# A decoder trunk on one core: attention scores of two units issued by turns into two banks

## The chip, the cores and the metric

The kernel runs on one core of one Trainium2 chip. The metric is the device time of the whole program in microseconds (us). Three runs of the kernel before took 1552.73, 1553.09 and 1553.78 us; their median is 1553.09.

The core has engines that work side by side, each through its own list of instructions in a fixed order: PE (matrix products and transposes, with PEld for its weight loads), DVE (vectors), ACT (functions of one operand, copies), POOL, and SP, which here only issues DMA transfers. A result of PE lies in one of eight banks of PSUM, each 128 rows of 512 fp32 numbers, and has to be read from there by DVE or ACT. An engine that meets an instruction whose operand or whose bank is not ready waits, and all that is behind it in its list waits too.

## The reference

The program computes a trunk of two decoder layers for 256 tokens of 1024 numbers in fp32. Each layer has attention with two groups of eight heads, an output projection, and a feed-forward part: dense in layer 0, eight experts with the best two for each token in layer 1.

```python
for layer in range(DEPTH):
    u = rmsnorm(h, attn_norm[layer])
    proj = u @ w_in[layer]
    ...
    o_a = nsa_mixer(...)        # group A: compressed + selected + window branch, gated
    o_b = dilated_mixer(...)    # group B
    o = jnp.concatenate([rmsnorm(o_a, ...), rmsnorm(o_b, ...)], axis=-1)
    h = h + o @ w_out[layer]
    v = rmsnorm(h, ffn_norm[layer])
    h = h + (swiglu(...) if layer % 2 == 0 else moe_swiglu(...))
```

The scores of one head are the products of its 256 queries with its keys, 64 numbers each, plus a bias that depends on the distance; then comes exp, and the product with the values. In group A a head has two such branches with the same queries (selected and window), and a third one on 15 keys that come from a small network over windows of 32 tokens (the compression).

## The kernel before

The 256 tokens are two tiles t = 0, 1 of 128 rows. Weights come in pieces of 1 MB through four raw slots (`N_RAW`), in the order of one list (`Weights`, L94 and L95 split each half-piece into a high part `whi`, by ACT, and a low part `wlo`, by DVE). A slot is loaded again when its last reader has run. Products with weights are made of three fp32r products each (`product3`, L366 to L368): `pj` for the input projection, `y` for the output projection, `eg`, `eu`, `ey` for the experts.

`attention` makes the projections in chunks: three for group A, then three for group B (`B_CHUNKS`: keys, queries, values). Right behind the first chunk of group B the list of weights has the four pieces of `cmp_w1` (1 MB each), which the compression reads whole, unsplit.

A group is worked off in units (`branch`). A unit fills one bank with scores (`sc`): at t=0 four heads or branches of 128 keys, at t=1 two of 256 keys. Its front is, for each of the two or four, a sum with the bias and the row minimum on DVE (L481, into `ns`, with `mn`) and exp on ACT (L483). Its back is four transposes on PE (`pT`, L490) into a bank, and a copy to `pt`, by ACT and DVE in turn (L493, L495). Its last step is eight products with the values (`o`, L502). In group A two heads that share a unit's place differ in g, and head g reads the rows g*64 to g*64+63 of queries and keys; so units alternate between the halves of the rows. In group B it is r that alternates.

The banks of PSUM: three under the tag "mm" (projections), two under "tr" (all transposes, and the scores), two under "acc" (`o`), one under "cmp". The compression (`compress`, from L537) has its steps in "cmp": `xt` (transposes of keys and values, L541), eight additions `xp` on DVE (L549), `hid` (128 products into strips of 32 columns, L559), then `hidT`, `kvc`, `kcT`. `combine` (L510 to L527) scales a branch's output and adds it up in `oa`.

The program text is not the order of the engines. A scheduler walks through the steps by its own estimate of when each is ready and when a bank or a slot comes free, and writes each engine's list; where a tag has fewer banks than steps that want one, the step that comes first in the text gets it.

Of the kernel before, what the change touches and what calls it, by code (L numbers as in the profile page):

```python
# [2 lines left out]

# [7 lines left out]
F32 = mybir.dt.float32  # L11
# [10 lines left out]
S = 256  # L22
# [15 lines left out]
# columns of the packed constant array  # L38
C_ID, C_TRI, C_IOTA, C_BDM, C_VALID, C_END = 0, 128, 256, 386, 394, 396
# rows of the packed vectors  # L40
# [12 lines left out]
class Weights:  # L53
    """Weight tiles: loaded in the order of the list, fp32 in, an exact sum of two fp32r parts out."""
# [25 lines left out]
    def take(self):  # L80
        """The two parts of the next piece, for each of its blocks of 128 rows."""
# [5 lines left out]
        out = []  # L87
# [13 lines left out]
def trunk_kernel(ctx: ExitStack, tc: tile.TileContext, T: dict, out: bass.AP):  # L101
# [23 lines left out]
    BANKS_A = (tr_bank,)  # L125
    BANKS_B = (tr_bank, cmp_bank)

    # ---------------------------------------------------------------- weights
# [52 lines left out]
    # the experts' pieces also go where attention has finished  # L181
# [3 lines left out]
    # -------------------------------------------------------------- constants  # L185
# [64 lines left out]
    # ones, and ones where the row is before the column: exact in bf16  # L250
# [5 lines left out]
    # distance bias, negated, and the mask, as rows over distance + 255  # L256
    scr = dram.tile([16, 512], F32, name="scr")

    def bias_rows(apool):
        oh = apool.tile([32, 512], F32, name="oh", tag="ns", bufs=2)  # L260
        pool.dma_start(out=oh, in_=T["c_onehot"])
        cn = apool.tile([16, 512], F32, name="cn", tag="ns", bufs=2)
# [7 lines left out]
    # ---------------------------------------------------------------- helpers  # L270
    def rsqrt(ms, shape, name):
        """1/sqrt(ms), by Newton's steps from an integer guess."""
# [17 lines left out]
    def row_rstd(src, n, name):  # L290
        """rstd of each token over the n columns of src[t]."""
# [6 lines left out]
    def split_psum(hi, lo, src, scale=None):  # L298
        """src * scale = hi + lo, both fp32r."""
# [8 lines left out]
    def transpose_split(src, row, l, hi, lo, ks):  # L308
        """hi + lo [128, k, S] = gain * transpose of the column blocks of src[t], blocks ks of the gain."""
# [9 lines left out]
    def lift(row, l, c0, cw, hi, lo):  # L319
        """Columns c0 ... of h, transposed, for the product that follows the norm of this row."""  # L320
        ks = range(c0 // 128, (c0 + cw) // 128)
        k = slice(ks[0], ks[-1] + 1)
        transpose_split([h[t][:, c0:c0 + cw] for t in range(NT)], row, l, hi[:, k, :], lo[:, k, :], ks)

    def turn_h(c0, cw, ht):
        """Columns c0 ... of h, transposed."""
# [12 lines left out]
    def residual(c0, cw, y, scale=None):  # L339
        """Columns c0 ... of h += scale * y[t]."""  # L340
# [12 lines left out]
    def column_groups(c, fine):  # L353
        """The groups of columns in which half c of h is computed: smaller ones where the next phase waits for them."""
        return [(0, 256), (256, 256)] if fine and c == 1 else [(0, 512)]

    def out_banks(bank, cw):
        """One output of cw columns for each token tile."""
# [5 lines left out]
    def product3(dst, xh, xl, wh, wl, first, last):  # L364
        """dst += (xh + xl) (wh + wl) to fp32's accuracy."""
# [3 lines left out]

    def dense(dst, hi, lo, cw):  # L370
        """dst[t][:, :cw] = (hi + lo)^T @ the next two weight tiles."""
# [6 lines left out]
    # -------------------------------------------------------------- attention  # L378
    def attention(l, apool, hi, lo, following):
# [7 lines left out]
        # row p begins one column further on: the columns run from the last key to the first  # L387
# [10 lines left out]
        # the projections: of group A the queries, the rest; of group B the queries and keys, the values  # L398
# [14 lines left out]
        def head_rstd(src, n, name, scale=None):  # L413
            """rstd of each of the n heads of src[t], times scale."""
# [14 lines left out]
        def norm_heads(dst, pj, c0, name, paired=False):  # L429
            """The eight heads of dst[t], each scaled by its rstd; paired: heads i and 4 + i side by side."""  # L430
# [13 lines left out]
        def norm_keys():  # L444
            """The selected and the window keys of group A, scaled by their rstd, in place."""
# [8 lines left out]
        def heads_t(dst, pj, c0, n, scale):  # L454
            """dst [128, n, S], or its two parts: n pairs of heads of pj, transposed and scaled."""
# [13 lines left out]
        def branch(units, t, scores, vpj, tbl, banks):  # L469
            """Causal attention of the units: lists of (head, column of v, output, denominators)."""  # L470
# [3 lines left out]
            def front(u, k):  # L474
                b = banks[k % len(banks)]("sc")
# [657 lines left out]
```

## Time and profile before

| | |
|---|---|
| median of three runs | 1553.09 us |
| profiled execution, first to last instruction | 1555.6 us |
| PE busy | 1527.9 us (98%) |
| DVE, ACT busy | 1235.4 us (79%), 1026.8 us (66%) |
| mean granted clock of PE | 0.993 |
| read from memory | 433.92 MB |

The attention of layer 0 lies between about 20 and 165 us, that of layer 1 between about 390 and 525 us; from about 535 us on it is the experts. The granted clock is a share of full speed: 1.00 is 2.4 GHz, 0.50 is 1.2 GHz. The rows of the section below have the start and the length of a group of instructions in us; a product's shown length includes what the next one overlaps, so the time that it takes is read from its start to the start of the next. In square brackets stands how long the engine had been idle, and for what.

### The profile page before, as it was taken

The page shows a single profiled execution, that of the slowest core. Times are in us where ns is not written, and L with a number is a line of the kernel's source. Part 1 is how long each engine was busy: PE and PEld are TensorE (multiplying, and loading weights), DVE is VectorE, ACT ScalarE, POOL GpSimd, SP SyncE. Part 2 cuts the span into 40 slices and gives each one's busy share as a digit, 9 for nine tenths or more (in the row PEclk, how much of TensorE's full clock was granted, in tenths as well). Part 3 has the DMA queues.
Part 4 walks back from the last instruction along what each step waited for, and adds up shares of the span by engine and source line. Part 5 has one row for each costly group of instructions (what it writes and reads, how often), then busy time and mean ns, then how long its engine had stood idle before and what let it go on. Part 6 is the DMA issues. An engine that isn't in the chain of part 4 may idle for free.

```text
span 1555.6 us, 20636 instructions
## 1 busy us (share of the span) xinstructions
PE 1527.9 (98%) x7502; PEld 1234.2 (79%) x7502; DVE 1235.4 (79%) x1771; ACT 1026.8 (66%) x1389; POOL 7.8 (1%) x17
## 2 busy tenths in 40 slices
PE   7999999999999999999999999999999999999997
PEld 6767888888777888888888878887887887887885
DVE  5567755555766798998998888988888889888886
ACT  5445644445545587887787777767777776767774
POOL 2000000000000000000000000000000000000000
PEclk9999999999999999999999999999999999999999
DMA  8812455557626499999999989999999999999980
GB/s 263 292 55 82 157 178 177 200 189 234 229 96 217 167 357 331 379 357 329 361 363 333 363 320 336 344 356 342 326 370 352 327 358 346 329 352 365 353 323 29
DMA packets 200907, 436.94 MB, mean 281 GB/s; under 512 B 9448, under 2 KB 26080, under 8 KB 200800
## 3 DMA queue, kind: packets, MB, share of 16 engines
q1 hardware_dynamic: 198160, 434.63, 79.2%
q8 instruction: 61, 1.00, 0.3%
q10 hardware_dynamic: 2176, 0.52, 0.2%
q0 software_dynamic: 464, 0.40, 0.1%
q14 instruction: 46, 0.38, 0.1%
HBM read 433.92 MB, written 1.08 MB: 280 GB/s over the span
## 4 chain that ended last, share of the span: by engine, by line
PE 95%; DMA 2%; DVE 2%; ACT 1%; issue 1%; SPq 0%; ACTq 0%; DVEq 0%
PE eu L368 7%; PE eg L368 7%; PE eu L367 6%; PE eu L366 6%; PE eg L367 6%; PE eg L366 6%; PE ey L366 6%; PE ey L367 6%; PE ey L368 6%; PE pj L368 3%; PE pj L366 3%; PE pj L367 3%; PE y L368 2%; PE y L367 2%; PE y L366 2%; PE o L502 2%
## 5 line engine op out<-in xcount | busy, mean ns | idle before, releaser
L95 DVE TENSOR_TENSOR wlo<-raw,whi 128x1024 fp32r<-128x1024 f32 (+1 forms) x802 | 946.1, 1215 | 158.9 <-ACT whi L94 147.9
L94 ACT ACTIVATE whi<-raw 128x1024 fp32r<-128x1024 f32 (+1 forms) x802 | 807.0, 1051 | 188.7 <-PE y L367 45.2
L368 PE MATMUL eg<-wlo,xe 128*128 128x512 f32 x448 | 177.4, 396 | 1.5 <-DVE wlo L95 1.5
L368 PE MATMUL eu<-wlo,xe 128*128 128x512 f32 x448 | 178.6, 399 | 0.0
L366 PE MATMUL ey<-whi,eth 128*128 128x512 f32 x448 | 177.5, 397 | 0.7 <-ACT eth L301 0.7
L366 PE MATMUL eg<-whi,xe 128*128 128x512 f32 x448 | 176.8, 395 | 0.7 <-ACT xe L304 0.3
L366 PE MATMUL eu<-whi,xe 128*128 128x512 f32 x448 | 177.4, 396 | 0.0
L367 PE MATMUL ey<-whi,etl 128*128 128x512 f32 x448 | 176.8, 395 | 0.0
L367 PE MATMUL eg<-whi,xe 128*128 128x512 f32 x448 | 175.9, 393 | 0.0
L367 PE MATMUL eu<-whi,xe 128*128 128x512 f32 x448 | 175.2, 391 | 0.0
L368 PE MATMUL ey<-wlo,eth 128*128 128x512 f32 x448 | 165.7, 399 | 0.0
L368 PEld LDWEIGHTS eu<-wlo,xe 128*128 128x128 f32 x448 | 84.1, 188 | 23.9 <-DVE wlo L95 6.9
L368 PEld LDWEIGHTS eg<-wlo,xe 128*128 128x128 f32 x448 | 84.2, 188 | 22.4 <-DVE wlo L95 4.6
L366 PEld LDWEIGHTS ey<-whi,eth 128*128 128x128 f32 x448 | 84.3, 188 | 20.7 <-ACT eth L301 1.1
L367 PEld LDWEIGHTS ey<-whi,etl 128*128 128x128 f32 x448 | 84.5, 189 | 20.2 <-DVE etl L302 0.4
L366 PEld LDWEIGHTS eg<-whi,xe 128*128 128x128 f32 x448 | 84.2, 188 | 20.3 <-ACT whi L94 2.6
L367 PEld LDWEIGHTS eg<-whi,xe 128*128 128x128 f32 x448 | 84.1, 188 | 17.8
L367 PEld LDWEIGHTS eu<-whi,xe 128*128 128x128 f32 x448 | 84.2, 188 | 17.1
L366 PEld LDWEIGHTS eu<-whi,xe 128*128 128x128 f32 x448 | 84.2, 188 | 15.8
L368 PEld LDWEIGHTS ey<-wlo,eth 128*128 128x128 f32 x448 | 82.5, 188 | 17.4
L301 ACT ACTIVATE eth<-eT 128x512 fp32r<-128x512 f32 x56 | 33.1, 592 | 88.7 <-PE ey L368 75.0
L366 PE MATMUL pj<-whi,uhi 128*128 128x512 f32 (+1 forms) x192 | 76.3, 399 | 0.8 <-ACT qv L411 0.8
(299 smaller groups left out, 1970.5 us busy)
## 6 DMA issues: line engine op xcount, KB each, us to landing
raw<-in_exp_w_gate_dram SPq DMA_DIRECT2D x112, 1024.0 KB, 7.0
raw<-in_exp_w_up_dram SPq DMA_DIRECT2D x112, 1024.0 KB, 7.0
raw<-in_exp_w_down_dram SPq DMA_DIRECT2D x112, 1024.0 KB, 6.8
raw<-in_w_in_dram SPq DMA_DIRECT2D x20, 1024.0 KB, 6.0
raw<-in_ffn_w_gate_dram SPq DMA_DIRECT2D x10, 1024.0 KB, 5.1
raw<-in_ffn_w_up_dram SPq DMA_DIRECT2D x10, 1024.0 KB, 5.2
raw<-in_ffn_w_down_dram SPq DMA_DIRECT2D x10, 1024.0 KB, 5.1
raw<-in_cmp_w_dram SPq DMA_DIRECT2D x8, 1024.0 KB, 6.2
```

The lines of the kernel that those rows point to most:

```text
L94: self.nc.scalar.activation(hi[:, :m * w], src, AF.Copy)
L95: self.nc.vector.tensor_tensor(out=lo[:, :m * w], in0=src, in1=hi[:, :m * w].bitcast(F32), op=ALU.subtract)
L301: act.activation(hi, src, AF.Copy)
L366: pe.matmul(dst, xh, wh, start=first, stop=False)
L367: pe.matmul(dst, xl, wh, start=False, stop=False)
L368: pe.matmul(dst, xh, wl, start=False, stop=last)
L502: pe.matmul(o[:, hd * HD:(hd + 1) * HD], pt[:, c:c + 128], vpj[:, j, vc:vc + HD], start=(j == 0), stop=(j == nj - 1))
```

## The change

Units are taken in pairs. The scores of both are issued first, step by step by turns, one unit into a bank of "tr" and the other into "cmp", for group A as for group B; then come both fronts, then for each unit its back and its last step. Group A's scores had "tr" alone before. The two units of a pair lie in different halves of the rows. `ns` has four buffers instead of two. The count of instructions of each kind stays the same, and so do their sizes.

```diff
-    BANKS_A = (tr_bank,)
+    BANKS_A = (tr_bank, cmp_bank)
...
+    def product3_by_steps(dst, xh, xl, wh, wl):
+        yield partial(pe.matmul, dst, xh, wh, start=True, stop=False)
+        yield partial(pe.matmul, dst, xl, wh, start=False, stop=False)
+        yield partial(pe.matmul, dst, xh, wl, start=False, stop=True)
...
-            def front(u, k):
-                b = banks[k % len(banks)]("sc")
-                ns = apool.tile([128, 512], F32, name="ns", tag="ns", bufs=2)
+            def products(us, k):
+                bs = [banks[(k + i) % len(banks)]("sc") for i in range(len(us))]
+                for step in zip(*[scores(b, u) for b, u in zip(bs, us)]):
+                    for mm in step:
+                        mm()
+                return bs
+
+            def front(u, b):
+                ns = apool.tile([128, 512], F32, name="ns", tag="ns", bufs=4)
                 mn = apool.tile([128, 4], F32, name="mn", tag="mn", bufs=3)
-                scores(b, u)
...
-            for k, u in enumerate(units):
-                _, ns = front(u, k)
-                last(u, back(ns, k))
+            for k in range(0, len(units), 2):
+                us = units[k:k + 2]
+                fronts = [front(u, b) for u, b in zip(us, products(us, k))]
+                for i, u in enumerate(us):
+                    last(u, back(fronts[i], k + i))
```

`scores` yields its products now instead of issuing them, in group A by `product3_by_steps`. The new lines move all line numbers behind them; L485 of the new kernel is the line that issues the scores.

What the scheduler makes of it is shown at three places of PE's list in layer 0. The first is the first scores of group A, before (`sc_513` is the bank of the first unit, `pj_1024` a bank of the first projection of group B):

```order
L366 MATMUL pj_1024<-whi_1029,uhi_93 128x512
L367 MATMUL pj_1024<-whi_1029,ulo_94 128x512
L368 MATMUL pj_1024<-wlo_1030,uhi_93 128x512
L366 MATMUL sc_513<-kta_425,qta_424 128x256
L367 MATMUL sc_513<-kta_425,qta_424 128x256
L366 MATMUL pj_1024<-whi_1029,uhi_93 128x512
L368 MATMUL sc_513<-kta_425,qta_424 128x256
```

and after (`sc_513` is the unit in "tr", `sc_514` its partner):

```order
L368 MATMUL pj_1024<-whi_1057,ulo_94 128x512
L485 MATMUL sc_513<-kta_425,qta_424 128x256
L485 MATMUL sc_514<-kta_425,qta_424 128x256
L485 MATMUL sc_513<-kta_425,qta_424 128x256
L485 MATMUL sc_514<-kta_425,qta_424 128x256
```

The twelve products of the first pair stand by turns. The second place is a unit at t=1 in the middle of group A, before (`o0_637` and `o1_638` are the outputs of the two branches, `pj_1115` a bank of group B's second projection):

```order
L490 MATMUL pT_693<-cc_70,ns_684 128x128 x2
L366 MATMUL sc_704<-kta_425,qta_424 128x512
L490 MATMUL pT_693<-cc_70,ns_684 128x128 x2
L367 MATMUL sc_704<-kta_425,qta_424 128x512
L368 MATMUL sc_704<-kta_425,qta_424 128x512
L367 MATMUL pj_1115<-whi_1157,ulo_94 128x512
L368 MATMUL pj_1115<-wlo_1158,uhi_93 128x512
L502 MATMUL o0_637<-pa_209,pt_698 128x64 x2
L502 MATMUL o1_638<-pa_209,pt_698 128x64 x2
L366 MATMUL pj_1115<-whi_1157,uhi_93 128x512
```

and after, the end of the last pair's scores (`sc_768` is the unit in "cmp", `sc_767` the one in "tr") and what follows:

```order
L502 MATMUL pT_756<-cc_70,ns_739 128x128 x2
L485 MATMUL sc_768<-kta_425,qta_424 128x512
L514 MATMUL o0_637<-pa_209,pt_750 128x64 x2
L514 MATMUL o1_638<-pa_209,pt_750 128x64 x2
L502 MATMUL pT_756<-cc_70,ns_739 128x128 x2
L485 MATMUL sc_767<-kta_425,qta_424 128x512 x3
L514 MATMUL o0_637<-pa_209,pt_761 128x64 x2
L514 MATMUL o1_638<-pa_209,pt_761 128x64 x2
L502 MATMUL pT_787<-cc_70,ns_775 128x128 x4
L555 MATMUL xt_821<-cc_70,kv_281 128x128 x3
```

The two units' scores stand one after the other here, the partner in "cmp" first; no projection stands between, and `xt` follows the last scores. The third place is the beginning of `hid`, before, where what an instruction waits for stands in brackets (`raw_839` and `raw_841` are pieces of `cmp_w1`):

```order
L366 MATMUL pj_1023<-whi_1057,uhi_93 128x512 [waits Activation_49]
L367 MATMUL pj_1023<-whi_1057,ulo_94 128x512
L559 MATMUL hid_834<-raw_839,xp0_176 32x128 [waits DMAHW2_49,DVE_49,PE_49]
L559 MATMUL hid_834<-raw_839,xp0_176 32x128
L368 MATMUL pj_1023<-wlo_1058,uhi_93 128x512 [waits DVE_49]
```

and after, from the end of `hid` to the first projection behind it:

```order
L573 MATMUL hid_834<-raw_877,xp1_177 32x128 x2
L579 MATMUL hidT_913<-cc_70,hs_911 128x128 [waits Activation_49]
L597 MATMUL kvc_925<-w2_151,gelu_915 32x64 [waits DMASW1_49,DVE_49,PE_49]
L597 MATMUL kvc_925<-w2_151,gelu_915 32x64
L599 MATMUL kvc_925<-w2_151,gr_922 128x64 [waits DVE_49] x2
L367 MATMUL pj_1115<-whi_1119,uhi_93 128x512 [waits Activation_49]
```

`hid` stood inside the first projection of group B and ahead of all scores of A; now it stands behind A's last `o`, and the second projection of group B (`pj_1115`) begins only behind it.

## Rows read from the trace of the kernel before

**Rows 1.** The page, chain of waits: shares of the span by engine.

```profile
PE 95%; DMA 2%; DVE 2%; ACT 1%; issue 1%; SPq 0%; ACTq 0%; DVEq 0%
```

**Rows 2.** Windows: width, busy time and (count) of each engine, granted clock, DMA share, GB/s.

```profile
400.00:450.00 50.00, 49.98 (x365) 35.65 (x364) 34.52 (x137) 26.62 (x80) 0.00 (x0) 1.00 0.36 127
600.00:700.00 100.00, 100.00 (x450) 82.02 (x449) 93.18 (x85) 80.97 (x85) 0.00 (x0) 1.00 1.00 366
```

**Rows 3.** Timeline of PE: start, length, line, result<-operands, shape, count; first scores.

```profile
62.25 0.28 PE L366 MATMUL sc<-kta,qta 64*128 64x256 f32 x1
62.37 0.27 PE L367 MATMUL sc<-kta,qta 64*128 64x256 f32 x1
...
62.69 1.07 PE L559 MATMUL hid<-raw,xp 128*32 128x128 f32 x30
```

**Rows 4.** Timeline of PE, a unit at t=1.

```profile
92.30 0.38 PE L490 MATMUL pT<-cc,ns 128*128 128x128 f32 x2
92.61 0.49 PE L366 MATMUL sc<-kta,qta 64*128 64x512 f32 x1
93.03 0.44 PE L490 MATMUL pT<-cc,ns 128*128 128x128 f32 x2
93.40 0.50 PE L367 MATMUL sc<-kta,qta 64*128 64x512 f32 x1
93.74 0.39 PE L368 MATMUL sc<-kta,qta 64*128 64x512 f32 x1
94.06 0.50 PE L367 MATMUL pj<-whi,ulo 128*128 128x512 f32 x1
...
94.64 1.00 PE L502 MATMUL o<-pa,pt 128*128 128x64 f32 x8
95.45 0.48 PE L366 MATMUL pj<-whi,uhi 128*128 128x512 f32 x1
```

**Rows 5.** Windows, three short stretches.

```profile
52.00:56.00 4.00, 4.00 (x41) 2.48 (x42) 3.86 (x17) 0.00 (x0) 0.00 (x0) 0.57 0.78 217
98.00:108.00 10.00, 9.91 (x38) 7.21 (x37) 5.28 (x16) 3.68 (x13) 0.00 (x0) 0.66 0.01 1
154.00:158.00 4.00, 4.00 (x27) 3.19 (x26) 3.48 (x7) 2.44 (x7) 0.00 (x0) 1.00 0.28 56
```

**Rows 6.** Timeline of PE, the two waits in layer 0.

```profile
50.21 0.41 PE L559 MATMUL hid<-raw,xp 128*32 128x128 f32 x4 [0.85 <-issue]
51.45 0.50 PE L368 MATMUL pj<-wlo,uhi 128*128 128x512 f32 x1 [0.83 <-DVE wlo L95]
```

**Rows 7.** Timeline of all engines, one unit (CUSTOM_DVE is the sum).

```profile
98.09 0.42 DVE L481 CUSTOM_DVE_ANT_0 ns<-sc,ta 128x256 f32<-128x256 f32 x1 [0.26 <-PE sc L368]
...
99.13 0.49 ACT L483 ACTIVATE ns<-ns,mn 128x256 f32<-128x256 f32 x1
...
99.35 0.44 PE L490 MATMUL pT<-cc,ns 128*128 128x128 f32 x2
...
101.41 0.69 DVE L495 COPY pt<-pT 128x512 f32<-128x512 f32 x1 [0.63 <-PE pT L490]
...
102.02 0.79 PE L366 MATMUL pj<-whi,uhi 128*128 128x512 f32 x1
...
104.75 1.80 PE L502 MATMUL o<-pa,pt 128*128 128x64 f32 x8
```

**Rows 8.** Timeline of DVE, an xp addition; and a combining product.

```profile
46.36 0.27 DVE L549 TENSOR_TENSOR xp<-xt,gv 128x120 f32<-128x120 f32 x1
...
119.86 0.69 DVE L524 TENSOR_TENSOR oa<-o,cf 128x512 f32<-128x512 f32 x1
```

**Rows 9.** The page: costliest groups (ACT whi), DMA issues (w_in).

```profile
L94 ACT ACTIVATE whi<-raw 128x1024 fp32r<-128x1024 f32 (+1 forms) x802 | 807.0, 1051 | 188.7 <-PE y L367 45.2
...
raw<-in_w_in_dram SPq DMA_DIRECT2D x20, 1024.0 KB, 6.0
```

**Rows 10.** Timeline of PE, group B's first scores.

```profile
142.70 1.71 PE L690 MATMUL sc<-qktb 64*128 64x128 f32 x16
```

More of the change, by code (lines that the diff above doesn't have):

```diff
@@ L2 @@
 from contextlib import ExitStack
+from functools import partial
 import numpy as np
@@ L259, in bias_rows @@
     def bias_rows(apool):
-        oh = apool.tile([32, 512], F32, name="oh", tag="ns", bufs=2)
+        oh = apool.tile([32, 512], F32, name="oh", tag="ns", bufs=4)
         pool.dma_start(out=oh, in_=T["c_onehot"])
-        cn = apool.tile([16, 512], F32, name="cn", tag="ns", bufs=2)
+        cn = apool.tile([16, 512], F32, name="cn", tag="ns", bufs=4)
         pool.dma_start(out=cn, in_=T["c_neg"])
@@ L484, in front @@
                                    accum_out=den[:, hd:hd + 1])
-                return u, ns
+                return ns
             def back(ns, k):
@@ L660, in scores @@
                         c = slice(t * 128, (t + 1) * 128)
-                        product3(b[:, i * J:(i + 2) * J].rearrange("p (b j) -> p b j", b=2), qh[p, qi, c], ql[p, qi, c],
-                                 kh[p, :, 0:J], kl[p, :, 0:J], True, True)
+                        yield from product3_by_steps(b[:, i * J:(i + 2) * J].rearrange("p (b j) -> p b j", b=2),
+                                                     qh[p, qi, c], ql[p, qi, c], kh[p, :, 0:J], kl[p, :, 0:J])
                 n = 2 // (t + 1)
@@ L689, in scores @@
                         p = slice(r * 64, r * 64 + 64)
-                        pe.matmul(b[:, i * J:(i + 1) * J], qt[p, qi, t * 128:(t + 1) * 128], kt[p, qi, 0:J],
-                                  start=True, stop=True)
+                        yield partial(pe.matmul, b[:, i * J:(i + 1) * J], qt[p, qi, t * 128:(t + 1) * 128],
+                                      kt[p, qi, 0:J], start=True, stop=True)
                 units = [[(2 * (u * n + i) + r, (2 * (u * n + i) + r) * HD, o, den) for i in range(n)]
```

## The prediction

> **What bounds the kernel now.** I read the page's chain of waits first [rows 1]: 95% of the chain that ended last is the own work of the matrix engine, PE. So time is won or lost where PE's work becomes shorter or longer, or where PE stands still. The table of windows says where that is [rows 2]: in the experts (600 to 700 us) PE works 100.00 of 100 us while the DMA engines are as full, and in the attention of layer 1 (400 to 450) it works 49.98 of 50. There is next to no idle time in the attention for a change to take away, and whatever it delays reaches the end, since nothing behind it has slack. What can shrink is PE's work itself: the scores, and the cost of going from one kind of product to another.
>
> **The products by turns.** The scores take 64 rows of the array, and two units that lie in different halves could run together. How many are left side by side is told by the order of the changed program, not by the diff: in group A the first pair at t=0 alternates (12 products), in group B the first pair (8). Every later pair stands unit after unit, because the bank "cmp" comes free before the next bank of "tr", so the unit that has it is scored first. That makes 20 of 64 products per layer. Do halves overlap at all? No row of before has two products of different halves side by side. The nearest are the 30 hid products in strips of 32 columns, 1.07 us for all, 36 ns each, against 0.11 to 0.12 us for one score of 256 columns [rows 3]; so parts of the array do work together, and I take it for rows too. The bounds are nothing, and half of the alternated products: 12 x 0.11 / 2 = 0.65 us in A, and in B 16 records in 1.71 us, half of it 0.85 [rows 10]. I take 1.5 us saved per layer. Had all products alternated, it would be about 4.0 (24 of 0.11 and 24 of 0.22 us in A, halved) and 2.55 in B, 13 us for both layers.
>
> The Trainium skill ("TensorEngine Tiling (Array Packing)", section "Theoretical Speedup") gives up to 2x for a contraction of at most 64, which agrees with that bound; no row here shows it. The same page (section "PSUM Bottleneck") says that tiling speeds up the products and not the emptying of the banks, which speaks against this change: by it the 13 us would be had only where the softmax behind the scores is not what the next unit waits for.
>
> **Fewer changes of shape.** Between the first score and the last o, before changes between kinds of product 58 times (hid, projection, score, transpose, o), after 33 times. One change costs what the rows of a unit show over the back-to-back time: a score of 512 columns takes 0.42 us to the next row instead of 0.22 (twice the 256 columns of [rows 3]), two transposes 0.37 instead of 0.21 (0.107 for 128 columns, [rows 10]), the next scores 0.34 and 0.32 [rows 4]: 0.20, 0.16, 0.12 and 0.10 more, on average 0.145. 25 x 0.145 = 3.6 us, and some 8 changes less where hid ran in bits ahead of that, 1.2 us: 4.8 us saved per layer.
>
> **What the second bank moves.** This is the large term. "cmp" was the bank of the compression; now the scores of A hold it. In before xt and hid stand in the middle of the projections, ahead of the scores. In after xt is placed behind the last pair's scores and hid behind the last o. The four tiles of cmp_w1 that hid reads are 1 MB each and fill all four raw slots, since they come before the weights of group B's second and third projection. So those weights cannot be fetched until hid has run, and 63 of the 70 projection products that lie between A's units in before are simply not there: after the first 7 the order shows none until hid is done. The products are no cheaper later, but the units have lost their cover. Per layer:
>
> - A unit at t=1 without cover is 2.57 us of PE work: transposes 0.31 and 0.37, scores 0.42, 0.34 and 0.32, o 0.81 [rows 4]. While one unit's chain runs (first sum on DVE to the end of the second exponential 1.53 us, two last transposes 0.44, copy 0.69, hand-overs 0.1: 2.8) [rows 7], PE has only the other unit's 2.57. It falls short by about 0.3 per unit, 0.6 per pair; bounds 0 and a whole 2.8. Three pairs: 1.8 us.
> - The first t=1 pair: DVE has the two combining products of t=0 (0.69 each) [rows 8] between the two sums of that pair's first unit, where they wait for the last o of t=0. 2.2 us, and the pair's 0.6. The second t=0 pair, with four short heads in a chain: 1.0.
> - Before hid: the last two copies with nothing else for PE, 1.9; then eight xp additions (0.27 each, 0.2 in a row) with three combining operations among them (0.69, 0.6 in a row), 3.4 in all, and while they run PE still has about 0.55 of its last o: 2.85 [rows 8].
> - After hid: the slots of the first two tiles are freed half-way, when 64 x 36 ns = 2.3 us of hid are left. A w_in tile lands 6.0 us after its issue and its first part is made in 1.05 [rows 9]; 6.0 + 1.05 - 2.3 = 4.75, less 0.6 of transposes and small products: 4.1. On SP's queue the w_out loads stand behind these w_in loads and move with them; nothing else that PE waits for in this stretch is queued there.
>
> 1.8 + 2.8 + 1.0 + 1.9 + 2.85 + 4.1 = 14.5 us of new idle time per layer. The same waits in reverse are what before loses in layer 0 by having hid early: PE idle for 0.85 and 0.83 us [rows 6], then a clock of 0.57 over 4 us, and 0.66 over 98 to 108 us [rows 5]. That is 1.7 + 0.43 x 4 + 0.34 x 10 = 6.8 us, which goes, since those places look different. In layer 1 before has no such loss.
>
> **The clock.** Before's clock was at the lower level, 1.2 GHz, in 100 to 106 us, after a stretch from 96 on in which no projection stood; and it was not in 154 to 158 us, in group B, where none stood either [rows 5]. After has some 35 us of A without a projection, twice, and then two waits. Bounds: only the tail and the first projections slow, 2 us per layer; or the whole stretch. At the lower clock the transposes and scores of a unit took 2.67 us (99.35 to 102.02) instead of 1.76, and o 1.80 instead of 1.00 as shown [rows 4, 7]: 4.15 us instead of 2.57, so a pair goes from 5.76 to about 8.3; with four such pairs, two at t=0, hid and the first projections it is 20 us per layer. The units of A and B are alike, B's kept 1.00 and A's at 100 us fell; I take 7.5 us, a third of the way, since A's units after the change follow each other with only 0.6 of 5.76 us idle.
>
> The Trainium skill ("TensorE: Matmul & The Clock Gate", section "Part 4: PE-mode transpose") says that transposes do not count as PE being busy in the same way, so these units (a quarter transposes) would count for less. The rows of B at 1.00 neither bear that out nor exclude it.
>
> **The sum**, against the profiled execution's own span of 1555.6 us, 2.5 us above the median of the runs (1553.09), which I take off again at the end. Layer 0: +14.5 - 4.8 - 1.5 - 6.8 + 7.5 = +8.9. Layer 1: +14.5 - 4.8 - 1.5 + 7.5 = +15.7. The experts are full, so both reach the end: +24.6, 1580.2 in the profile, **1578 us** against the median. No instruction is added or taken away, and DVE, ACT and POOL have the same work; only waits move.
>
> **The rivals.**
> *The clock stays up* (2 us per layer): 1567 us. For it: group B's stretch. Against: 100 to 106 us. Chance 0.22.
> *The clock falls early and stays* (20 us per layer): 1603 us. For it: the fall at 100 us came in such a stretch and lasted until projections ran again. Against: group B. Chance 0.17. The Trainium skill's rule on transposes, named above, would have it go this way.
> *Faster*: the two halves run together and their fewer changes of shape pay, while the waits are covered by the second bank: with two units' scores ready, PE always has one unit's transposes while the other's softmax runs. Then the 7.5 us of waits at the units and their last copies go, the tail's 2.85 + 4.1 stay, the clock holds, and the sum per layer is 7.0 - 4.8 - 6.5, less 6.8 once: -8.6 and -6.8, 1538 us with all products overlapping, and 1548 with the 20 that the order leaves (1.5 in place of 6.5). It decides from where the new waits are under 4.8 + 1.5 + 3.4 = 9.7 us per layer. For it: the order does have two units in flight. Against: before had 70 projections for the same purpose and hardly ever stood still [rows 2]. Chance 0.08.
> *The change does nothing it says*: halves do not overlap and only the order changes. The time is then 3 us more, 1581, within the forecast's own case, since the terms that decide do not hang on it. A balance of waits and savings that ends within 3 us of 1553: 0.06.
>
> **How the numbers follow.** The forecast's own case (1570 to 1592): 0.47. With the rivals that is 0.22 + 0.17 + 0.08 + 0.06. A measurement tells about 0.2% (3.1 us) from no change. Faster 0.08, same 0.06, slower 0.86. The range reaches from 1562, which is 1567 less the units' own waits of 1.8 and 1.0 in both layers, to 1606, the half-clock case with 3 us for its own spread; 0.14 lies below it and some 0.05 above.
>
> **What would show it.** In the profile after: scores of both units at less than 0.11 us spacing in the first pair only; no projection between A's units; xt and hid after the last scores; PE's idle time before hid put down to DVE xp, and behind it to ACT whi; about 14 us of idle time per layer; the lower clock in part of the stretch; in layer 0, SP's w_in loads of group B only after hid has begun. The forecast is wrong if the loads land before hid ends, if the pairs' chains are longer than their rows say, or if the lower clock takes all of the stretch or none.

## The result and the profile after

The changed kernel took 1599.91 us (median of 4 runs, 1598.25 to 1600.74) against 1553.43 for the kernel before (4 runs, 1552.73 to 1555.72): a ratio of 1.0292 [1.0278, 1.0307], 46 us slower. The forecast was 1578 with a range to 1606, and slower. The direction, the place and the chain of causes hold; the sum is 22 us short. The term that made it so is the clock, which is 38 us too small over both layers; the idle time, 13 us too large, hides a third of that. The cause is also narrower than the change: the second bank alone, without pairs and without turns, costs 41 us, and the intervals do not tell whether the other 5 are more than noise.

The profiled execution spans 1597.5 us, 41.9 more than before. That is less than the 46 us between the medians, because the profiled execution of the kernel before was a long one: a run's time on record is about 2.2 us more than the span of its core, so its span of 1555.6 stands for some 1558 us, 4 above the median. From the page of after: busy time, the granted clock of PE in 40 slices, and the chain of waits by engine, which answers to [rows 1].

```profile
PE 1554.9 (97%) x7502; PEld 1258.7 (79%) x7502; DVE 1240.2 (78%) x1771; ACT 1027.0 (64%) x1389; POOL 7.8 (0%) x17
...
PEclk9859999999958989999999999999999999999999
...
PE 93%; DVE 2%; DMA 2%; ACT 1%; issue 1%; SPq 0%; ACTq 0%
```

PE is still nearly all of the chain. Its busy time grew by 27.0 us (1527.9 before) and its idle time by the other 14.9, so most of the 42 us are work that PE does more slowly. The two dips of the clock row are the attention of the two layers. Three markers say where the time went in. The first product of the dense FFN (fg) starts 17.8 us later than before (197.3 against 179.5), the first product of the experts (eg) 42.3 us later (576.9 against 534.6), and the end comes 41.9 us later: the experts hand on all they receive, as the prediction said of them.

Windows from the first score of group A to that next stage, for layer 0 and layer 1. The columns are from:to, width, busy us of PE (count), PEld, DVE, ACT and POOL, granted clock, DMA share, GB/s. First the kernel before:

```profile
61.17:179.50 118.33, 117.15 (x684) 88.89 (x684) 79.21 (x267) 63.84 (x167) 0.00 (x0) 0.97 0.33 111
406.85:534.60 127.75, 123.81 (x715) 96.99 (x714) 86.34 (x301) 67.64 (x173) 0.00 (x0) 0.97 0.51 178
```

and after, with two parts of layer 0 beside them:

```profile
57.55:120.65 63.10, 56.29 (x342) 42.07 (x341) 25.72 (x117) 20.70 (x74) 0.00 (x0) 0.63 0.09 32
68.00:104.00 36.00, 34.50 (x118) 24.06 (x118) 12.91 (x54) 10.74 (x37) 0.00 (x0) 0.50 0.00 1
...
57.55:197.30 139.75, 130.50 (x745) 101.11 (x744) 81.64 (x274) 63.15 (x166) 0.00 (x0) 0.82 0.28 98
423.42:576.90 153.48, 141.23 (x820) 112.04 (x820) 90.22 (x309) 67.84 (x173) 0.00 (x0) 0.82 0.44 151
```

In layer 0 the first score starts 3.6 us earlier and the stretch behind it is 21.4 us longer. Idle time grew from 1.18 to 9.25 us (width less PE's busy time): 8.1. What the clock cost is worked out as (1 - clock) x width: 0.18 x 139.75 = 25.2 us against 0.03 x 118.33 = 3.5, so 21.7 more (high by up to about 3, since idle time at the lower clock is in it). What is left, 21.4 - 8.1 - 21.7 = -8.4 us, is what PE's own work became shorter. It is a remainder, so it takes up the errors of the other two. Layer 1 in the same way: 25.7 = 8.3 idle + 23.8 clock - 6.4.

The second window of after is the heart of it: over 36 us the clock is 0.50, the lower of its two levels, while PE is busy for 34.50 of them. No projection stands in that stretch; the last one before it starts at 60.45.

### The profile page after: what moved, and what is told of

It is laid out like the page before. It is cut to its first block, busy times and chain, and to the rows that moved or that the text cites. A ratio compares the mean times of both kernels' runs of the same rounds, so it can differ in the third digit from the quotient of the medians.

```text
span 1597.5 us, 20625 instructions
## 1 busy us (share of the span) xinstructions
PE 1554.9 (97%) x7502; PEld 1258.7 (79%) x7502; DVE 1240.2 (78%) x1771; ACT 1027.0 (64%) x1389; POOL 7.8 (0%) x17
## 4 chain that ended last, share of the span: by engine, by line
PE 93%; DVE 2%; DMA 2%; ACT 1%; issue 1%; SPq 0%; ACTq 0%
PE eu L369 7%; PE eu L368 6%; PE eu L367 6%; PE eg L369 6%; PE eg L368 6%; PE eg L367 6%; PE ey L367 6%; PE ey L368 6%; PE ey L369 6%; PE o L514 3%; PE sc L485 3%; PE pj L368 2%; PE pj L369 2%; PE pj L367 2%; PE y L368 2%; PE y L369 2%
## 5 line engine op out<-in xcount | busy, mean ns | idle before, releaser
L369 PEld LDWEIGHTS eu<-wlo,xe 128*128 128x128 f32 x448 | 84.1, 188 | 23.8 <-DVE wlo L96 6.9
L367 PEld LDWEIGHTS eu<-whi,xe 128*128 128x128 f32 x448 | 84.2, 188 | 15.7
```

The costliest lines, as they stand in the source:

```text
L367: pe.matmul(dst, xh, wh, start=first, stop=False)
L369: pe.matmul(dst, xh, wl, start=False, stop=last)
```

## The experiments

**What of the change costs the time?** First the bank alone, in the kernel before: no pairs, no turns, `ns` as it was.

```diff
-    BANKS_A = (tr_bank,)
+    BANKS_A = (tr_bank, cmp_bank)
```

> The kernel before with one line changed: group A's scores use the banks of "tr" and "cmp", unit after unit, without pairs and turns. Theory (the second bank moves the compression behind the scores of A, the projections lose their slots until it has run, and PE is left with units alone, which wait and drop the clock): about the time of the changed kernel, +40 to +50 us, 1593 to 1603 us. Rival (pairs are what costs: two fronts stand ahead of the first back, so the chain of a unit is longer): the bank alone costs little, 1553 to 1563 us.

Measured: 1594.01 us (1593.12 to 1599.32), ratio 1.0277 [1.0252, 1.0301], as expected. The window of its layer 0:

```profile
57.00:120.00 63.00, 55.67 (x331) 41.15 (x330) 26.75 (x116) 21.78 (x77) 0.00 (x0) 0.64 0.10 35
```

It is the same stretch as in after: 7.3 us idle, clock 0.64. Then the other half, the changed kernel with its pairs and turns but with group A in the banks of "tr" alone:

```diff
-    BANKS_A = (tr_bank, cmp_bank)
+    BANKS_A = (tr_bank,)
```

> The changed kernel with group A's scores in the two banks of "tr" alone: pairs and turns stay, "cmp" is the compression's again. Theory (the compression's place decides): the compression stands early again, projections lie between A's units, and the time is near that of the kernel before, 1548 to 1560 us; the turns themselves are worth 1 to 2 us per layer, the waits of transposes for a "tr" bank that scores hold take some of it back. Rival (pairs cost): most of the loss stays, 1580 to 1600 us.

Measured: 1542.61 us (1542.09 to 1543.64), ratio 0.9936 [0.9919, 0.9952], faster than expected. Window and timeline of PE (start, length, line, result<-operands, rows*columns of the array, shape, count):

```profile
60.00:100.00 40.00, 39.33 (x283) 29.60 (x283) 27.80 (x117) 23.45 (x76) 0.00 (x0) 1.00 0.41 142
59.79:170.10 110.31, 108.14 (x684) 84.56 (x684) 79.05 (x267) 63.18 (x167) 0.00 (x0) 1.00 0.35 119
...
91.97 0.97 PE L485 MATMUL sc<-kta,qta 64*128 64x512 f32 x6
92.86 0.50 PE L368 MATMUL pj<-whi,ulo 128*128 128x512 f32 x1
```

hid is back among the first scores, projections run between the units, the clock is 1.00, and the DMA engines are at work again (142 GB/s against 1 in the stretch of after). The six products of a pair take 0.89 us to the next row. The second window is that of its layer 0 from first score to fg: PE works 108.14 us there at clock 1.00, in before 117.15 less the 3.5 that the clock cost, so its own work is 5.5 us shorter. The bank costs 41 us without pairs, and pairs without the bank gain 10. The two do not add up: pairs on top of the bank gain nothing (1599.91 against 1594.01).

**Is it the raw slots?** The prediction's chain was: compression late, so its four weight tiles hold all four slots, so no projections. Two ways to cut it with the second bank kept. The first runs the compression ahead of group A:

```diff
-COMPRESS_FIRST = False
+COMPRESS_FIRST = True
```

> The changed kernel with the compression written ahead of A's scores, so that it gets the bank "cmp" first; pairs, turns and both banks for A stay. Theory: slots come free early, 25 and more projections lie between A's units, no lower clock over tens of us; 1545 to 1558 us. Rival (pairs cost): 1575 to 1600 us.

Measured: 1576.58 us (1573.81 to 1579.2), ratio 1.0151 [1.0129, 1.0173], outside what the theory gave. It lies in the rival's range, but the rival's reason (pairs cost) does not hold: pairs without the bank had gained. The second loads the compression's weights after two more of the projection's:

```diff
-W1_AFTER = 0
+W1_AFTER = 2
```

> The changed kernel with the compression's weights at the end of the projections' weights instead of behind the first chunk of group B, so that they hold no slot while B's other weights are wanted; the compression still comes behind A's scores. If it is the slots through which the bank hurts (no projections between the units, so waits and the lower clock), the loss is nearly gone: 1552 to 1565 us, with the compression's own chain of some 5 us per layer partly uncovered. If the late compression hurts by its own chain, which everything behind waits for, most of the loss stays: 1580 to 1600 us.

Measured: 1590.27 us (1590.15 to 1590.61), ratio 1.0243 [1.0226, 1.026]. The slots alone would have given 1552 to 1565; it is the other case, the late compression that hurts by its own chain. First the windows of the run that compresses first, a score of group A's first pair, and two waits at the end of its group A (in square brackets PE's idle time before the row, and who ended it):

```profile
60.00:100.00 40.00, 37.04 (x213) 27.38 (x213) 23.37 (x91) 18.90 (x52) 0.00 (x0) 0.83 0.49 168
100.00:140.00 40.00, 37.39 (x205) 27.42 (x203) 25.61 (x80) 18.32 (x49) 0.00 (x0) 1.00 0.25 79
...
78.67 1.51 PE L485 MATMUL sc<-kta,qta 64*128 64x256 f32 x6 [0.64 <-ACT kct L619]
...
133.94 0.33 PE L641 MATMUL cpT<-cc,cp 128*128 128x128 f32 x1 [1.23 <-ACT cp L637]
...
141.56 0.69 PE L316 MATMUL ut<-cc,oa 128*128 128x128 f32 x2 [1.40 <-DVE oa L541]
```

and the run with the later loads:

```profile
60.00:100.00 40.00, 40.00 (x207) 28.05 (x205) 26.10 (x95) 22.05 (x70) 0.00 (x0) 1.00 0.35 106
100.00:140.00 40.00, 29.92 (x264) 24.85 (x264) 21.08 (x72) 11.41 (x26) 0.00 (x0) 0.82 0.44 158
...
129.86 0.28 PE L613 MATMUL kcT<-cc,kc 32*128 32x32 f32 x1 [7.97 <-DVE kc L611]
130.78 3.62 PE L626 MATMUL cs<-kct,qta 128*128 128x32 f32 x16 [0.64 <-ACT kct L619]
135.87 0.48 PE L641 MATMUL cpT<-cc,cp 128*128 128x128 f32 x1 [1.47 <-ACT cp L637]
```

The slots are the reason why the projections are missing: with them freed, PE works 40.00 of 40 us of group A at full clock. But the loss only moves. The projections are now spent on group A, and the compression, which still waits for its bank until A is done, runs with nothing beside it: 7.97 us for one chain through DVE, and the clock falls here instead. With the compression first, the second unit of group A's first pair waits for the bank: its scores start at 78.67, behind the compression's last copy (`kct`), when its partner's had started at 59.74; and later steps lack cover. So the slots are one way in which the loss appears, and the shared bank is behind each: "cmp" has two users now, and in both runs the one that came first made the other late.

**Is it the clock?** To hold PE's activity up without the projections, each unit of group A in the changed kernel got one full product of 128x512 into a bank that is already read out; its result is not used. That is 24 products over both layers, 0.86 us each to the next row at full clock (63.84 to 64.70), some 21 us.

```diff
+                if fill:
+                    pe.matmul(b, pt[:, 0:128], vpj[:, 0, 0:512], start=True, stop=True)
                 return pt
...
-                branch(units, t, scores, pa, ta, BANKS_A)
+                branch(units, t, scores, pa, ta, BANKS_A, True)
```

> The changed kernel with one product more per unit of group A (128 rows by 512 columns in fp32, 0.86 us at the full clock, into the bank of the unit's transposes once they are copied; its result isn't used). 24 such products in all, 21 us of work at the full clock, 41 at half. Theory (in the stretch without projections PE falls to the lower clock, and that is the larger part of the loss): with more work between the transposes the clock stays up or falls later, and the time is below or near the changed kernel's although there is more work: 1585 to 1605 us. If the clock is not what costs, or does not hang on how much the products work: 1620 to 1642 us.

Measured: 1595.13 us (1588.09 to 1601.97), ratio 1.027 [1.0226, 1.0315]: 21 us of added work, and not slower than the changed kernel. Its four runs are the longer the lower their mean granted clock is, from 1588.09 us at 0.989 to 1601.97 at 0.980. Windows, first of three parts, then of both layers from the first score to the next stage, and the row behind the first part:

```profile
60.00:84.00 24.00, 22.99 (x117) 14.99 (x115) 13.49 (x67) 10.93 (x44) 0.00 (x0) 1.00 0.00 0
84.00:108.00 24.00, 23.15 (x63) 13.58 (x63) 5.45 (x26) 6.92 (x25) 0.00 (x0) 0.55 0.00 1
420.00:450.00 30.00, 29.72 (x159) 19.96 (x157) 17.51 (x78) 13.72 (x49) 0.00 (x0) 1.00 0.00 1
58.91:199.80 140.89, 132.75 (x768) 97.97 (x768) 81.61 (x274) 63.05 (x166) 0.00 (x0) 0.90 0.28 98
425.85:576.30 150.45, 137.07 (x844) 104.73 (x844) 90.26 (x309) 67.92 (x172) 0.00 (x0) 0.93 0.44 154
...
84.79 0.93 PE L502 MATMUL pT<-cc,ns 128*128 128x128 f32 x4 [1.16 <-ACT ns L495]
```

The clock holds to 84 us where it fell at 68 in the changed kernel, and in layer 1 over the whole of 420 to 450 us (there 0.50 from 440 on). Then it goes, within 3 us of the wait at 84.79, and from 84 to 108 us it is mostly at the lower level although the dense products stand in these units too; whether that wait brings it down, no run shows. The added products did not simply fill idle time: over both layers PE idles 21.5 us with and without them, while what the clock costs falls from 52.8 to 24.6 us ((1 - clock) x width, as above), by more than was added. So for a time the same units, without projections and without DMA traffic, run at full clock when a dense product is among them: the clock is a cause of its own and not a by-product of the missing loads.

**Do the turns do anything?** The kernel with pairs in "tr", its scores issued unit after unit:

```diff
-                for step in zip(*[scores(b, u) for b, u in zip(bs, us)]):
-                    for mm in step:
+                for b, u in zip(bs, us):
+                    for mm in scores(b, u):
                         mm()
```

> As e2_turns_in_tr (pairs, A's scores in the banks of "tr" alone), but the scores of a pair are issued unit after unit, not by turns. Theory: in the changed kernel's trace the turns save what the first pairs show, 0.3 us per layer in A and 0.5 in B, and e2's gain of 10 us comes from pairs (fewer changes of shape, two units in flight under projections): 1542 to 1546 us. Rival (the turns bring the gain): 1550 to 1555 us, the kernel before's time.

Measured: 1544.4 us (1539.15 to 1545.24), ratio 0.9954 [0.9938, 0.9971], as expected.

```profile
88.42 0.98 PE L485 MATMUL sc<-kta,qta 64*128 64x512 f32 x6
89.32 0.66 PE L599 MATMUL kvc<-w,gr 128*128 128x64 f32 x4
...
130.52 1.71 PE L485 MATMUL sc<-qktb 64*128 64x128 f32 x16
```

Six products of two units, three and three, take 0.90 us, as with turns. In group B the sixteen records without turns take 1.64 us to the next row, as in before (length 1.71, [rows 10]); by turns, in the changed kernel, they take 1.10 (length 1.16). To see the overlap itself, a kernel of blocks of 24 products (fp32r) and 16 (fp32, two records each, not shown below): all in one half, by turns in both, three and three, and full products with half ones by turns.

```diff
+    def block(name, n, halves, width, x=q, y=k, each=1):
+        bs = [mm_bank(name) for _ in halves]
+        for i in range(n):
+            j = i // each % len(halves)
+            p = slice(*halves[j])
+            pe.matmul(bs[j][:, 0:width], x[p, 0:128], y[p, 0:width], start=True, stop=True)
```

> Not the trunk: blocks of 16 or 24 score-like products alone (the rest of the computation is left out), with 128-row products of 512 columns between them. In turn, for fp32r with 512 and 256 columns: all in the lower half of the rows into two banks; lower and upper half by turns; three of one half and three of the other. Then fp32 with 256 and 128 columns, same half and by turns; last, 128-row and 64-row products by turns. Theory (halves overlap, but only partly): same half 0.22 us per product of 512 and 0.11 of 256; by turns 0.16 to 0.20 and 0.08 to 0.10; fp32 by turns a third less than same half; three and three between them. Rival (halves run fully side by side): by turns half the time. Rival (no overlap): the same time. The alternation of 128 and 64 rows shows what a change of shape costs: 0.1 to 0.2 us over a product's own time.

Its timeline of PE at clock 1.00, of 512 columns; what a block takes is read from its start to the next row's:

```profile
26.45 5.75 PE L1067 MATMUL rsame<-k,q 64*128 64x512 f32 x24
32.13 3.01 PE L1067 MATMUL warm<-k,q 128*128 128x512 f32 x12
35.07 3.04 PE L1067 MATMUL rturn<-k,q 64*128 64x512 f32 x24
38.04 3.04 PE L1067 MATMUL warm<-k,q 128*128 128x512 f32 x12
41.01 3.04 PE L1067 MATMUL rthree<-k,q 64*128 64x512 f32 x24
43.99 3.02 PE L1067 MATMUL warm<-k,q 128*128 128x512 f32 x12
...
90.31 10.20 PE L1067 MATMUL mix<-k,q 128*128 128x512 f32 x24
100.45 1.85 PE L1067 MATMUL warm<-k,q 128*128 128x512 f32 x7
```

5.68 us in one half, 2.97 by turns and 2.98 three and three: the halves run almost fully side by side, as the rival said, and with three in a row turns are not needed for it. The single starts in the trace say the same: the first product of the other half starts 0.003 us behind the first of its own by turns, and 0.010 us behind it in three and three, long before three products are through. With eight records each in a row, in group B without turns, a second series starts only 0.55 us behind the first, and little of it overlaps.

Then pairs and turns in one group alone. Group B, in the kernel whose group A goes unit by unit in "tr":

```diff
+            n_us = 1 if banks is BANKS_A else 2
-            for k in range(0, len(units), 2):
-                us = units[k:k + 2]
+            for k in range(0, len(units), n_us):
+                us = units[k:k + n_us]
```

> The kernel before with pairs and turns in group B alone; group A unit after unit in "tr" as before (with four ns buffers). Theory (turns halve a pair's scores where both banks are free at once): only B's first pair per layer stands by turns, 0.55 us saved there per layer as its 16 records take 1.16 us instead of 1.71, and two units in flight change little else, since output projections lie between: 1548 to 1552 us, 1 to 3 us faster than before. Rival (e2's gain of 10 us comes from group B): 1542 to 1546 us.

Measured: 1555.3 us (1554.09 to 1560.26), ratio 1.0023 [1.0012, 1.0034], where a gain was expected. PE at the end of group B:

```profile
162.01 0.87 PE L316 MATMUL ut<-cc,ob 128*128 128x128 f32 x6 [0.67 <-DVE ob L713]
163.13 0.96 PE L367 MATMUL y<-whi,pob 128*128 128x512 f32 x4 [0.24 <-ACT pob L305]
```

Neither wait stands in the kernel before, and 0.67 + 0.24 is more than the 0.55 us saved at the scores. That leaves 0.4 us per layer, while the medians lie 2.5 us apart; where the rest comes from was not found. And group A alone, with the condition turned round:

> As e2_turns_in_tr, with pairs and turns in group A alone; group B unit after unit as before. Theory: nearly all of e2's gain, 1542 to 1547 us. Rival: 1548 to 1552 us.

Measured: 1540.97 us (1540.84 to 1542.5), ratio 0.9926 [0.9911, 0.9941]: all of the gain. On the same chip as these two ran the kernel with turns in both groups and that without turns once more:

> e2_turns_in_tr, word for word, on the same chip as e12_no_turns. Theory (three products of one half and three of the other overlap as well as single turns do, as the blocks alone showed, so that turns add only B's 0.55 us per layer): 1542 to 1544 us, at most 2 us faster than e12_no_turns. Rival (turns matter in A too): 4 us and more faster.

> e4_pairs_no_turns, word for word, on the same chip as e11_turns: pairs, unit after unit. Theory: 1543 to 1546 us, within 2 us of e11_turns. Rival: 1547 us and more.

Measured: 1539.88 us (1539.42 to 1541.91), ratio 0.9922 [0.9906, 0.9937], with turns; 1542.5 (1538.9 to 1545.22), ratio 0.9927 [0.9909, 0.9945], without. Both are a little faster than expected, and they are 2.6 us apart, between the 2 of the theory and the 4 of its rival; the intervals of the ratios lie on each other. Group A's pairs carry the gain, 6 to 13 us over the five runs with pairs in "tr", and turns add nothing that can be told apart. Four `ns` buffers do not bring it, since the run with pairs in group B alone had them too. How much of the gain is overlap and how much fewer changes of shape was not separated: counted in the trace, scores and hid products border on other kinds 56 times in layer 0 of before and 30 times with pairs in "tr", and at the prediction's 0.145 us these 26 would be 3.8 of the 5.5 us by which PE's work is shorter there (an estimate).

**Another bank instead?** The kernel with pairs and turns in "tr", with a third bank for "tr" that is taken from the projections:

```diff
-MM, TR, ACC = 3, 2, 2
+MM, TR, ACC = 2, 3, 2
```

> As e2_turns_in_tr, with three banks under "tr" and two under "mm": a pair's scores and a unit's transposes no longer want the same two banks. Theory: more pairs stand by turns and units wait less for banks, but a projection has to be emptied before the next one begins; 1538 to 1548 us. Rival (the projections wait for their banks): 1555 to 1570 us.

Measured: 1591.61 us (1590.66 to 1594.12), ratio 1.0262 [1.0244, 1.028]; slower, as the rival said, and 21 us beyond the rival's range.

```profile
58.23 0.69 PE L468 MATMUL ht<-cc,qv 128*128 128x128 f32 x2 [6.59 <-DVE qv L441]
```

DVE makes `qv` out of the two banks of a projection, and PE waits 6.59 us for it at this one place; with no third bank no projection of group B stands there (the first starts at 64.18). This bank can't be spared.

## Why the prediction was right in kind and short in size

| us per layer | predicted | layer 0 | layer 1 |
|---|---|---|---|
| new idle time | +14.5 | +8.1 | +8.3 |
| clock, against full speed | +7.5 | +25.2 | +27.6 |
| overlap and fewer changes of shape | -6.3 | -8.4 | -6.4 |
| what before loses already | -6.8, layer 0 alone | -7.1 (3.6 + 3.5) | -3.8 |
| sum | +8.9, +15.7 | +17.8 | +25.7 |

The first three rows and the 3.5 and 3.8 are those worked out above; the third is a remainder and takes up the errors of the others. In the fourth the agreement of 7.1 with 6.8 may be chance: the 3.6 us are the earlier first score, and two executions of one and the same program (e2_turns_in_tr and e11_turns) start it at 59.79 and 56.41 us. Layer 1's first score starts 1.2 us earlier than layer 0 hands on, so the experts start 24.5 us later by its part.

**The step that failed is the clock.** The term was 7.5 us per layer, and it measured 25.2 and 27.6. The prediction had bounds of 2 and 20 us and took a third of the way, because group B's units kept 1.00 without projections [rows 5] and because A's units would follow each other with little idle time. The second reason is what the run overthrows: in 68 to 104 us PE is busy for 96% and the clock is 0.50. Keeping busy did not keep the clock here. What PE works on matters: with one dense product per unit it held longer (1.00 to 84 us), though not to the end (0.55 from 84 to 108). The row of before that pointed this way was the fall at 100 us, and it was outvoted by four microseconds of group B. The right value was the upper bound and more, as in the rival "the clock falls early and stays", which gave 1603 and had 0.17; that is the case that came about. That its time comes so near is luck in part: over both layers its clock is 13 us too small (40 for 52.8) and its idle time 13 us too large (29 for 16.4). The upper bound was low in part because the row read for the lower clock, 99.35 to 102.02, has its first 0.6 us at full clock. Why group B's stretch stays at 1.00 is not settled.

The Trainium skill ("TensorE: Matmul & The Clock Gate", section "Part 4: PE-mode transpose") would have had it go this way, since by it transposes do not count as PE being busy in the same way. The trace of group A agrees with where that leads (0.50 with PE 96% busy), that of group B, with transposes at 1.00 [rows 5], does not show it. No run took the transposes alone away, so that it is they and not the half-row scores or the 64-column o products is not shown.

**The idle time was too large**, by 6 us per layer, partly for the same reason. A pair at the lower clock, timeline of PE in after:

```profile
85.03 1.06 PE L502 MATMUL pT<-cc,ns 128*128 128x128 f32 x4
86.02 1.22 PE L485 MATMUL sc<-kta,qta 64*128 64x512 f32 x2
...
90.83 1.65 PE L485 MATMUL sc<-kta,qta 64*128 64x512 f32 x3
92.41 1.97 PE L514 MATMUL o<-pa,pt 128*128 128x64 f32 x8
94.17 1.06 PE L502 MATMUL pT<-cc,ns 128*128 128x128 f32 x4
```

From one pair to the next it is 9.14 us (8.3 had been worked out) with no wait in it. The chain through DVE and ACT does not slow down with PE, so the slower PE covers it: the 1.8 us of the pairs became nothing, and the two terms should not have been added. The waits that remain in layer 0, PE's and one row of ACT:

```profile
76.65 0.69 PE L502 MATMUL pT<-cc,ns 128*128 128x128 f32 x2 [1.50 <-ACT ns L495]
...
107.27 1.10 PE L514 MATMUL o<-pa,pt 128*128 128x64 f32 x8 [0.75 <-ACT pt L505]
110.34 6.13 PE L573 MATMUL hid<-raw,xp 128*32 128x128 f32 x128 [1.96 <-issue]
116.89 0.33 PE L579 MATMUL hidT<-cc,hs 128*128 128x128 f32 x1 [0.42 <-ACT hs L577]
119.23 0.61 PE L597 MATMUL kvc<-w,gelu 128*32 128x64 f32 x4 [2.01 <-issue]
119.46 1.06 ACT L95 ACTIVATE whi<-raw 128x1024 fp32r<-128x1024 f32 x1 [0.65 <-DMA raw<-in_w_in_dram]
120.65 0.77 PE L367 MATMUL pj<-whi,uhi 128*128 128x512 f32 x1
```

The first t=1 pair: 1.50 for 2.8, behind the combining products as said. Before hid: 0.75 + 1.96 for 1.9 + 2.85, behind xp as said; the profile puts the second down to "issue", and DVE's last xp addition ends just before it. After hid: 0.42 + 2.01 for 4.1, and here the releaser was wrong. PE goes through hidT, gelu (on DVE and ACT) and kvc, a chain of small steps, and the first projection at 120.65 then finds its weights there, if only just: `whi` is done at 120.52. From the end of hid (116.47) to that projection it is 4.18 us where 4.75 had been worked out; but PE has 1.75 us of work on hidT and kvc in it, not 0.6. On SP's queue the loads do start only after hid has begun:

```profile
114.00 3.44 SPq L72 DMA_DIRECT2D raw<-in_w_in_dram  x4
```

but hid took 6.13 us, most of it at the lower clock, in place of 4.6, which gave the loads time. In layer 1 the same projection waited 0.23 us for ACT whi, so the margin is thin.

**The overlap** was sized somewhat high and argued badly. The prediction said that no row before has products of different halves side by side. [rows 10] is such a row: the first eight of its 16 records belong to one unit and the rest to another in the other half, 0.103 us each to the next row, and they hardly overlap. The first pair of the changed kernel, and group B's:

```profile
57.55 1.19 PE L485 MATMUL sc<-kta,qta 64*128 64x256 f32 x12
58.67 0.50 PE L369 MATMUL pj<-wlo,uhi 128*128 128x512 f32 x1
...
159.12 1.16 PE L485 MATMUL sc<-qktb 64*128 64x128 f32 x16
```

1.12 us for 12, 0.093 each against 0.11 to 0.12 [rows 3], some 0.3 us saved of a bound of 0.65; and 0.55 us saved in B of the 0.85 taken as its bound. That is 0.85 of the 1.5 us per layer. The blocks alone show nearly a full halving, in agreement with the Trainium skill ("TensorEngine Tiling (Array Packing)", section "Theoretical Speedup": up to 2x for half the rows); in the kernel the first pairs show part of it. The rival that halves do not overlap is refuted. Turns are not needed for the overlap where three products stand in a row; with eight records in a row they do matter (0.55 us in B).

**Changes of shape**: the 25 fewer per layer come out nearly so in the traces if only scores and hid products against all the rest are counted (56 and 31 times in layer 0, 53 and 33 in layer 1), and 0.145 us each was a fair price. In the block of full and half products by turns a product takes 0.4225 us to the next; its own time is between 0.23 and 0.25, so a change costs 0.17 to 0.19 us there. How the 8.4 and 6.4 us divide between overlap and changes was not taken apart.

**Faster**: the rival at 1538 to 1548 us was refuted for this change, but its numbers are those of the pairs in "tr" (1540 to 1544). That nearness is chance as far as is known: its sum has 7 us of new waits per layer, where the pairs in "tr" have about 1 (2.17 us idle against 1.18 in layer 0). What decided is what the text set against it, whether projections still stand between the units: there they do.

**In layer 1** the prediction said that before has no loss of its own. It has: clock 0.97 over 127.75 us, 3.8 us, most of it at the end of the stretch (0.94 over 480 to 534.6), where no row was read.

## What to carry to other kernels

Before a stage gets a second bank, a buffer or a queue, list who else uses it and see in the order produced what becomes late: here a bank given to the scores moved the compression, which held the load slots, which took the filling work from the very stage that was to gain. Price a stretch that loses its dense products at the lower clock from end to end, unless a row of the same work shows otherwise, since PE being busy did not keep the clock up here, and do not add waits that a slower PE covers. What paid here was to take the units of group A in pairs in the banks that the stage already has: 0.5 to 0.8%; whether it is the different halves or the fewer changes of shape that pay was not separated.

## What the runs showed of the hardware beyond what was expected

- PE's clock was at its lower level over 36 us in which PE was busy for 34.50; the work was transposes, products of 64 rows and products of 64 columns. With a product of 128 rows and 512 columns added to each unit the clock stayed at 1.00 to 84 us in layer 0 (68 without), and over all of 420 to 450 us in layer 1 (440 without); from 84 to 108 us it was 0.55 with these products too.
- Products in the two halves of the rows overlap almost wholly: 24 of 512 columns in 5.68 us in one half, 2.97 by turns and 2.98 three and three. Eight records and eight, in group B, hardly overlap (1.64 us to the next row), by turns much more (1.10).
- A change between products of 128 and of 64 rows costs 0.17 to 0.19 us each time (0.4225 us per product in place of 0.23 to 0.25).
